# Weight splits ordered behind activation splits at five stage ends of a two-layer trunk

## The chip, the core and the metric

The kernel runs on one core of a Trainium2 chip. The metric is the device time of one launch in microseconds (us); the kernel before takes 1660.06 us, the median of three runs. Engine names in the profile: PE is TensorE (matrix products and transposes), ACT is ScalarE, DVE is VectorE, POOL is GpSimd, SP is SyncE, which here only starts transfers from memory.

## What is computed

The input x has 256 tokens of 1024 float32 values. Two layers follow, each with three residual steps:

```
x = x + 0.5 * RMSNorm_post(SwiGLU_1(RMSNorm_pre(x)))
x = x +       RMSNorm_post(HybridMixer(RMSNorm_pre(x)))
x = x + 0.5 * RMSNorm_post(SwiGLU_2(RMSNorm_pre(x)))

swiglu(u) = (silu(u @ Wg) * (u @ Wu)) @ Wout          # 1024 -> 2 x 2816 -> 1024
HybridMixer(u): proj = u @ W_in, three branches (gated linear recurrence, retention with
  four heads, short convolution), each projected to 1024, summed with sigmoid gates, @ W_out
RMSNorm(x) = x * rsqrt(mean(x*x) + 1e-6) * g
```

So there are six stages in a row, FFN, mixer, FFN, FFN, mixer, FFN, and five places where one stage ends and the next begins. Each stage needs the whole normalised row of x before its first product.

## The kernel before, in words

All 256 tokens stay on the chip as two blocks of 128 rows, called tb 0 and tb 1. Only the weights are streamed in. They come in units of 128 x 1024 values, in one fixed order for the whole kernel, two units to a transfer of 1 MB.

Products are made in a split form: each operand is cut into a rounded high part and a low part that is the rest. `mm3` (lines 397 to 400) then makes three products that add up in one PSUM tile: activation high by weight high (line 398), activation high by weight low (399), activation low by weight high (400). So both weights and activations have to be split first:

- A weight unit is split in `Stream.prep`: ScalarE casts it to `whi` (line 155) and VectorE subtracts to get `wlo` (line 156). There are 8 buffers each for `whi` and `wlo`, and 3 for `raw`, each holding two units. `Stream.done` gives finished units back, and `fill` at once writes down the transfers, casts and subtractions of as many new units.
- Activations are turned by TensorE's transposes into a PSUM tile `pstr` (two of them, used in turn), and `split` casts on ScalarE (line 383) and subtracts on VectorE (line 384). For a stage's input the results are `uh` and `ul`, in two halves of four blocks each (`split_T`). For the last product of an FFN they are the two halves of `hl`.

An FFN step has 11 slices of 256 hidden columns. `fin` makes a slice's gate and up parts, `ftr` turns and splits the result, `fout` multiplies it with the output weights into `acc`. Of the last slice, e, the end of `ffn` goes in this order: for tb 0 `post` scales the sum and adds it to x, and `after` (which is `pre`) makes the next stage's normalised row: multiply by the gain (line 308), row scale, multiply (line 311). Then for tb 1 `fin(e)`, `fout(e-1)`, `ftr(e)`; then `turn`, the transposes of tb 0 for the next stage; `fout(e)`; and `post` and `pre` of tb 1. The transposes of tb 1 are made inside the next stage, at the sixth of eight steps of its second group of products (`inproj`, `KD - 3`).

A row scale (`rstd`) is squares on ScalarE (line 288), a sum on VectorE (line 292) and a power on GpSimd (line 293).

The end of a mixer is alike: `mix_out` multiplies with the last weights, four times for each tb, and `turn` of tb 0 stands inside the last one of tb 1.

In what follows n0 to n7 are the first eight weight units of the next stage. They take the buffers that the last units of the ending stage give back. In an FFN, n0 to n3 follow `fin(e, 1)`, n4 and n5 `fout(e-1, 1)`, n6 and n7 `fout(e, 1)`. In a mixer, two units follow each of the four `mix_out` of tb 1. The next stage's first group of products takes n0 to n3, its second n4 to n7, first for tb 0 and then for tb 1.

Each engine works through its own queue in order. The order in the queues is not that of the program text: a planner places every instruction when the program is built, on the free engine the ready one of highest priority first, by its own estimates of times. Priority is the place in the text; `high_priority(offset=CHAIN_LEAD)` moves an instruction ahead by 150 places.

Of the kernel before, what the change touches and what calls it, by code (L numbers as in the profile page):

```python
# [3 lines left out]

# [1 line left out]

# [5 lines left out]
F32 = mybir.dt.float32  # L12
# [3 lines left out]
ALU = mybir.AluOpType  # L16
# [103 lines left out]
class Stream:  # L120


    def __init__(self, nc, wpool, w, spare):
        self.nc, self.pool, self.w, self.spare = nc, wpool, w, spare
        self.plan = stream_plan()
        self.n = len(self.plan)
        self.next = 0
        self.pair = 0
        self.odd = False
        self.tiles = {}  # L130
        self.cur = 0
# [8 lines left out]
    def prep(self):  # L140
        nc, i = self.nc, self.next
        kind = self.plan[i]
        n = UW // 2 if i < FIRST else UW
        if kind is None:
            if not self.odd:
                self.raw = self.load(n if i < FIRST else 2 * UW)
            k0 = UW if self.odd else 0
            self.odd = not self.odd
            raws = [self.raw[:, k:k + n] for k in range(k0, k0 + UW, n)]
        else:  # L150
            raws = self.part(*kind)
        hi = self.pool.tile([P, UW], F32R, tag="whi", name=f"whi{i}", bufs=WBUFS)
        lo = self.pool.tile([P, UW], F32R, tag="wlo", name=f"wlo{i}", bufs=WBUFS)
        for k, raw in zip(range(0, UW, n), raws):
            nc.scalar.copy(hi[:, k:k + n], raw)  # L155
            nc.vector.tensor_sub(lo[:, k:k + n], raw, hi[:, k:k + n].bitcast(F32))  # L156
        self.tiles[i] = (hi, lo)
        self.next += 1

# [19 lines left out]
    def fill(self):  # L179
        lowest = min(self.tiles) if self.tiles else self.next  # L180
        while self.next < self.n and self.next - lowest < WBUFS:
            self.prep()

    def take(self, n):
        r = list(range(self.cur, self.cur + n))
# [15 lines left out]
def trunk_kernel(ctx: ExitStack, tc: tile.TileContext, x_in, pos, gains, gain0, par, id_in, consts, gw, w, out):  # L201
# [75 lines left out]
            return w4()  # L277
        return tp.tile([P, UW], F32, tag="spl", name=nm("gw"), bufs=7)

    st = Stream(nc, wp, w, spare)  # L280

    def rstd(parts, n, f=1.0):

# [15 lines left out]
    def halves(t):  # L299
        return [t[:, k * 512:(k + 1) * 512] for k in range(2)]  # L300

    def pre(tb, l, k, summed):


        xs = halves(x[tb])
        t = w4()
        for o, a, g in zip(halves(t), xs, halves(gain_tiles[(l, k)])):
            dve.tensor_mul(o, a, g)
        r = rstd([x[tb]], D)
        for o in halves(t):  # L310
            dve.tensor_scalar(o, o, r, None, op0=ALU.mult)

        def turn():
            split_T(tb, t, summed=summed)
        return turn


    sums = [None] * 2
# [2 lines left out]
    def sum_T(tb, j, pt):  # L321
        if tb == 0:
            if j == 0:
                whole[0] = w4()
            act.copy(whole[0][:, j * 512:(j + 1) * 512], pt)
        else:
            make_sums(j, whole[0][:, j * 512:(j + 1) * 512], pt)
# [12 lines left out]
    def split_T(tb, t, scale=None, summed=False):  # L340
        h = tp.tile([P, KD, P], F32R, tag=f"uh{tb}", name=nm("uh"))
        lo = tp.tile([P, KD, P], F32R, tag=f"ul{tb}", name=nm("ul"))
        uh[tb], ul[tb] = h, lo
        for j in range(2):
            pt = ps_tr()
            for i in range(4):
                c = 4 * j + i
                pe.transpose(pt[:, i * P:(i + 1) * P], t[:, c * P:(c + 1) * P], ident)  # L348
            with tc.high_priority(offset=CHAIN_LEAD):
                split(h[:, 4 * j:4 * j + 4, :], lo[:, 4 * j:4 * j + 4, :],  # L350
                      pt.rearrange("p (a b) -> p a b", a=4), scale)
            if summed:
                sum_T(tb, j, pt)

    def first(tb):

# [24 lines left out]
    def split(h, lo, src, scale=None):  # L381
        if scale is None:
            act.copy(h, src)  # L383
            dve.tensor_sub(lo, src, h.bitcast(F32))  # L384
        else:
            act.mul(h, src, scale)
            dve.scalar_tensor_tensor(lo, src, scale, h.bitcast(F32), op0=ALU.mult, op1=ALU.subtract)

    def post(tb, acc, l, k, f):
        r = rstd(acc, D, f)  # L390
# [11 lines left out]
    def inproj(us, tb, turn=None):  # L402

        ps = ps_in()
        for c in range(KD):
            if c == KD - 3 and turn is not None:
                turn()
            h, lo = st.get(us[c // 2])
            s = slice((c % 2) * 512, (c % 2 + 1) * 512)
            mm3(ps, uh[tb][:, c, :], ul[tb][:, c, :], h[:, s], lo[:, s], c == 0, c == KD - 1)  # L410
        return ps
# [20 lines left out]
    def ffn(l, kpost, after, turn, during=None, start=False):  # L432
# [6 lines left out]
        acc = [ps_acc() for _ in range(NTB)]  # L439

        def fin(s, tb, turn=None):
            gate_up(s, tb, [inproj(ui[s], tb, turn)])

        def gate_up(s, tb0, pss):
            for tb, ps in enumerate(pss, tb0):
                t = tok()
                with tc.high_priority(offset=CHAIN_LEAD if s == NS - 1 else 0):
                    act.activation(t[:, 0:256], ps[:, 0:256], AF.Silu)
                    dve.tensor_mul(t[:, 256:512], ps[:, 256:512], t[:, 0:256])
                hT[(s, tb)] = t  # L450

        def ftr(s, tb):
            t = hT[(s, tb)]
            pt = ps_tr()
            for i in range(2):
                pe.transpose(pt[:, i * P:(i + 1) * P], t[:, 256 + i * P:256 + (i + 1) * P], ident)  # L456
            hl = tp.tile([P, 2, 256], F32R, tag=("tmp", "tok")[tb], name=nm("hl"), bufs=(TMP, TOK)[tb])
            with tc.high_priority(offset=CHAIN_LEAD if s == NS - 1 else 0):
                split(hl[:, 0, :], hl[:, 1, :], pt[:, 0:256])
            hT[(s, tb)] = hl  # L460

        def fout(s, tb, ns=(0, 1)):
            hl = hT[(s, tb)]
# [120 lines left out]
        fout(e, 0)  # L584
        with tc.high_priority(offset=CHAIN_LEAD):
            post(0, acc[0], l, kpost, 0.5)
            turn = after(0)
        fin(e, 1)
        st.done(ui[e])
        fout(e - 1, 1)  # L590
        st.done(uo[e - 1])
        ftr(e, 1)
        if turn is not None:
            turn()
        fout(e, 1)
        st.done(uo[e])
        with tc.high_priority(offset=CHAIN_LEAD):
            post(1, acc[1], l, kpost, 0.5)
            return after(1)


    cosT = cp.tile([P, SEQ], F32, tag="cosT", name="cosT")
# [71 lines left out]
    def mixer(l, after, turn):  # L674
# [385 lines left out]
        def mix_out(tb, i, ns=(0, 1)):  # L1060
            outproj(macc[tb], [(uh[tb][:, j, :], ul[tb][:, j, :]) for j in (i, i + 1)],
                    umo[i:i + 2], i == 0, i == 6, ns)
# [4 lines left out]
                split_T(1, M[1], 0.5)  # L1067
        with tc.high_priority(offset=CHAIN_LEAD):
            post(0, macc[0], l, G_MPOST, 1.0)
            turn = after(0)  # L1070
        for i in range(0, 8, 2):
            mix_out(1, i, (0,))
            if i == 6:
                turn()
            mix_out(1, i, (1,))
            st.done(umo[i:i + 2])
        with tc.high_priority(offset=CHAIN_LEAD):
            post(1, macc[1], l, G_MPOST, 1.0)
            return after(1)


    first(0)
# [161 lines left out]
```

## Time and profile before

| what | value |
|---|---|
| median of three runs | 1660.06 us (1659.83 to 1660.34) |
| profiled execution | 1659.72 us |
| its span, first to last instruction | 1657.9 us |
| TensorE busy | 1643.6 us, 99% of the span |
| VectorE busy | 1245.4 us, 75% |
| ScalarE busy | 921.0 us, 56% |
| granted TensorE clock, mean | 0.998 |

The span is the time from the first to the last recorded instruction; the profiled execution has 1.8 us outside it. Matrix products overlap in TensorE, so a product of 0.39 us can start every 0.23 us; a gap in TensorE's work is therefore read from one start to the next and not from the busy time.

### The profile page before, as it was taken

What the parts mean: (1) busy time and instruction counts of PE and PEld (TensorE: products, weight loads), DVE (VectorE), ACT (ScalarE), POOL (GpSimd) and SP (SyncE); (2) the same over time, 40 slices, a digit from 0 to 9 for tenths busy, and PEclk for the clock granted to TensorE, in tenths of its full rate; (3) what the DMA queues carried; (4) which work ended last, traced back from release to release, by engine and by line L of the source; (5) the groups of instructions that cost most, each with busy time, mean ns of one, the idle gap of its engine ahead of it and who ended that gap; (6) DMA issues with size and microseconds to landing.
All of it is one profiled execution on the core that took longest, in us unless ns stands there. A gap on an engine that the chain in (4) does not pass through costs nothing.

```text
span 1657.9 us, 19700 instructions
## 1 busy us (share of the span) xinstructions
PE 1643.6 (99%) x7561; PEld 1354.4 (82%) x7561; DVE 1245.4 (75%) x1594; ACT 921.0 (56%) x1247; POOL 47.3 (3%) x71
## 2 busy tenths in 40 slices
PE   8999999999999999999999999999999999999998
PEld 6888788888888888888888888888888888888886
DVE  7878769976665657888689787798566566678784
ACT  6555567644544545655556555766445544465553
POOL 0030000000000000000000000000000000000000
PEclk9999999999999999999999999999999999999999
DMA  8553554555454465474465344645554454644621
GB/s 336 210 206 127 204 190 165 203 206 189 167 181 175 171 232 223 150 252 161 170 253 187 138 164 163 220 157 203 199 189 171 160 196 153 251 176 177 221 107 71
DMA packets 49774, 309.85 MB, mean 187 GB/s; under 512 B 5648, under 2 KB 6032, under 8 KB 17552
## 3 DMA queue, kind: packets, MB, share of 16 engines
q1 hardware_dynamic: 47376, 301.18, 49.6%
q10 hardware_dynamic: 2304, 7.41, 1.2%
q8 instruction: 59, 0.97, 0.2%
q14 instruction: 35, 0.29, 0.0%
HBM read 307.52 MB, written 1.05 MB: 186 GB/s over the span
## 4 chain that ended last, share of the span: by engine, by line
PE 95%; DVE 3%; issue 1%; POOL 1%; ACT 1%; DMA 0%; SPq 0%; DVEq 0%; POOLq 0%; ACTq 0%
PE psin L400 21%; PE psin L398 21%; PE psin L399 21%; PE psacc L400 9%; PE psacc L398 9%; PE psacc L399 9%; PE pstr L456 1%; DVE wlo L156 1%; PE pstr L713 1%; POOL small L293 1%; PE pstr L348 1%; DVE x L395 0%; PE pstr L881 0%; PE pstr L960 0%; DMA raw<-in_w_dram 0%
## 5 line engine op out<-in xcount | busy, mean ns | idle before, releaser
L156 DVE TENSOR_TENSOR wlo<-raw,whi 128x1024 fp32r<-128x1024 f32 (+1 forms) x506 | 603.7, 1215 | 250.0 <-ACT whi L155 241.6
L155 ACT CAST whi<-raw 128x1024 fp32r<-128x1024 f32 (+1 forms) x506 | 521.6, 1049 | 262.7 <-PE psacc L400 147.5
L398 PE MATMUL psin<-whi,uh 128*128 128x512 f32 x1440 | 567.7, 394 | 1.3 <-ACT uh L383 0.7
L400 PE MATMUL psin<-whi,ul 128*128 128x512 f32 x1440 | 562.5, 391 | 1.8 <-DVE ul L384 1.3
L399 PE MATMUL psin<-wlo,uh 128*128 128x512 f32 x1440 | 563.1, 391 | 0.0
L400 PEld LDWEIGHTS psin<-whi,ul 128*128 128x128 f32 x1440 | 270.6, 188 | 59.0 <-DVE ul L384 2.1
L398 PEld LDWEIGHTS psin<-whi,uh 128*128 128x128 f32 x1440 | 270.8, 188 | 57.4 <-ACT uh L383 2.0
L399 PEld LDWEIGHTS psin<-wlo,uh 128*128 128x128 f32 x1440 | 270.9, 188 | 53.4
L398 PE MATMUL psacc<-whi,hl 128*128 128x512 f32 x352 | 140.8, 400 | 0.8 <-ACT hl L383 0.5
L156 DVE TENSOR_TENSOR wlo<-gw,whi 128x1024 fp32r<-128x1024 f32 x96 | 115.9, 1219 | 30.6 <-ACT whi L155 30.6
L400 PE MATMUL psacc<-whi,hl 128*128 128x512 f32 x352 | 137.4, 392 | 0.0
L399 PE MATMUL psacc<-wlo,hl 128*128 128x512 f32 x352 | 137.4, 390 | 0.0
L155 ACT CAST whi<-gw 128x1024 fp32r<-128x1024 f32 x96 | 101.1, 1053 | 45.5 <-PE psin L400 24.9
L400 PE MATMUL psacc<-whi,spl 128*128 128x512 f32 x256 | 100.0, 391 | 0.0
L398 PE MATMUL psacc<-whi,spl 128*128 128x512 f32 x256 | 99.8, 390 | 0.0
L399 PE MATMUL psacc<-wlo,spl 128*128 128x512 f32 x256 | 99.7, 389 | 0.0
L400 PEld LDWEIGHTS psacc<-whi,hl 128*128 128x128 f32 x352 | 66.1, 188 | 15.2 <-DVE hl L384 1.3
L398 PEld LDWEIGHTS psacc<-whi,hl 128*128 128x128 f32 x352 | 66.1, 188 | 15.1 <-ACT hl L383 3.3
L399 PEld LDWEIGHTS psacc<-wlo,hl 128*128 128x128 f32 x352 | 66.2, 188 | 12.6
L293 POOL TENSOR_TENSOR small<-small,mhalf 128x1 f32<-128x1 f32 x40 | 28.9, 723 | 1534.6 <-DVE small L292 1533.7
L383 ACT CAST hl<-pstr 128x256 fp32r<-128x256 f32 x88 | 31.7, 370 | 56.5 <-PE pstr L456 56.5
L701 ACT COPY tok<-psin 128x512 f32<-128x512 f32 x40 | 23.5, 586 | 62.7 <-PE psin L400 62.7
(191 smaller groups left out, 1686.1 us busy)
## 6 DMA issues: line engine op xcount, KB each, us to landing
raw<-in_w_dram SPq DMA_DIRECT2D x251, 1024.0 KB, 4.8
gw<-in_w_dram SPq DMA_DIRECT2D x48, 512.0 KB, 6.9
w<-in_w_dram SPq DMA_DIRECT2D x16, 512.0 KB, 6.5
gain<-in_gains_dram ACTq DMA_DIRECT2D x10, 512.0 KB, 5.2
w<-in_gw_dram ACTq DMA_DIRECT2D x4, 512.0 KB, 3.5
x<-in_x_dram SPq DMA_DIRECT2D x2, 512.0 KB, 4.2
raw<-in_w_dram SPq DMA_DIRECT2D x4, 256.0 KB, 6.1
out_dram<-x SPq DMA_DIRECT2D x4, 256.0 KB, 2.0
```

Source lines behind the costliest of these rows:

```text
L155: nc.scalar.copy(hi[:, k:k + n], raw)
L156: nc.vector.tensor_sub(lo[:, k:k + n], raw, hi[:, k:k + n].bitcast(F32))
L293: pool_e.tensor_tensor(r, r, mhalf, op=ALU.pow)
L348: pe.transpose(pt[:, i * P:(i + 1) * P], t[:, c * P:(c + 1) * P], ident)
L383: act.copy(h, src)
L398: pe.matmul(ps, lhsT=xh, rhs=wh, start=first, stop=False)
L399: pe.matmul(ps, lhsT=xh, rhs=wl, start=False, stop=False)
L400: pe.matmul(ps, lhsT=xl, rhs=wh, start=False, stop=last)
L456: pe.transpose(pt[:, i * P:(i + 1) * P], t[:, 256 + i * P:256 + (i + 1) * P], ident)
L701: act.copy(t, ps)
L713: pe.transpose(pt[:, i * SEQ + tb * P:i * SEQ + (tb + 1) * P], toks[tb][:, c * P:(c + 1) * P], ident)
```

## The change

`tc.issue_after(ins)` is a block: every instruction written in it for the engine of `ins` gets an edge that puts it behind `ins` in that engine's queue. All the `ins` used here are VectorE's, so the edges bind VectorE's instructions alone; ScalarE's casts and the transfers of the same block are not bound, though they move to another place in the text.

- FFN end: `done(ui[e])` and `done(uo[e-1])` move from behind `fin(e, 1)` and `fout(e-1, 1)` to behind `ftr(e, 1)`, and the six `wlo` subtractions (n0 to n5) come behind the subtraction of `hl` (line 384).
- FFN end: `pre` is cut in two, and its last part (line 311) for tb 0 comes behind the product of gate and up (line 449) of `fin(e, 1)`.
- FFN end: `post` and `pre` of tb 1 come, on VectorE, behind the `wlo` subtraction of n3 (`behind(3)`).
- Mixer end: `done` of units 2 to 5 of the output weights moves behind `turn`, and the subtractions n2 to n5 come behind the last subtraction of `ul`. Units 0 and 1 (n0, n1) stay where they were.

```diff
--- before.py
+++ after.py
@@ -1,6 +1,6 @@
 import math
 from collections import deque
-from contextlib import ExitStack
+from contextlib import ExitStack, nullcontext
 
 import numpy as np
 
@@ -120,8 +120,9 @@
 class Stream:
 
 
-    def __init__(self, nc, wpool, w, spare):
-        self.nc, self.pool, self.w, self.spare = nc, wpool, w, spare
+    def __init__(self, tc, wpool, w, spare):
+        self.tc, self.nc, self.pool, self.w, self.spare = tc, tc.nc, wpool, w, spare
+        self.lows = {}
         self.plan = stream_plan()
         self.n = len(self.plan)
         self.next = 0
@@ -153,7 +154,7 @@
         lo = self.pool.tile([P, UW], F32R, tag="wlo", name=f"wlo{i}", bufs=WBUFS)
         for k, raw in zip(range(0, UW, n), raws):
             nc.scalar.copy(hi[:, k:k + n], raw)
-            nc.vector.tensor_sub(lo[:, k:k + n], raw, hi[:, k:k + n].bitcast(F32))
+            self.lows[i] = nc.vector.tensor_sub(lo[:, k:k + n], raw, hi[:, k:k + n].bitcast(F32))
         self.tiles[i] = (hi, lo)
         self.next += 1
 
@@ -181,6 +182,10 @@
         while self.next < self.n and self.next - lowest < WBUFS:
             self.prep()
 
+    def behind(self, k):
+
+        return self.tc.issue_after(self.lows[self.cur + k].ins) if self.cur + k < self.n else nullcontext()
+
     def take(self, n):
         r = list(range(self.cur, self.cur + n))
         self.cur += n
@@ -277,7 +282,7 @@
             return w4()
         return tp.tile([P, UW], F32, tag="spl", name=nm("gw"), bufs=7)
 
-    st = Stream(nc, wp, w, spare)
+    st = Stream(tc, wp, w, spare)
 
     def rstd(parts, n, f=1.0):
 
@@ -307,12 +312,16 @@
         for o, a, g in zip(halves(t), xs, halves(gain_tiles[(l, k)])):
             dve.tensor_mul(o, a, g)
         r = rstd([x[tb]], D)
-        for o in halves(t):
-            dve.tensor_scalar(o, o, r, None, op0=ALU.mult)
+
+        def scale(behind=None):
+
+            with tc.issue_after(behind.ins) if behind is not None else nullcontext():
+                for o in halves(t):
+                    dve.tensor_scalar(o, o, r, None, op0=ALU.mult)
 
         def turn():
-            split_T(tb, t, summed=summed)
-        return turn
+            return split_T(tb, t, summed=summed)
+        return scale, turn
 
 
     sums = [None] * 2
@@ -347,10 +356,11 @@
                 c = 4 * j + i
                 pe.transpose(pt[:, i * P:(i + 1) * P], t[:, c * P:(c + 1) * P], ident)
             with tc.high_priority(offset=CHAIN_LEAD):
-                split(h[:, 4 * j:4 * j + 4, :], lo[:, 4 * j:4 * j + 4, :],
-                      pt.rearrange("p (a b) -> p a b", a=4), scale)
+                last = split(h[:, 4 * j:4 * j + 4, :], lo[:, 4 * j:4 * j + 4, :],
+                             pt.rearrange("p (a b) -> p a b", a=4), scale)
             if summed:
                 sum_T(tb, j, pt)
+        return last
 
     def first(tb):
 
@@ -381,10 +391,9 @@
     def split(h, lo, src, scale=None):
         if scale is None:
             act.copy(h, src)
-            dve.tensor_sub(lo, src, h.bitcast(F32))
-        else:
-            act.mul(h, src, scale)
-            dve.scalar_tensor_tensor(lo, src, scale, h.bitcast(F32), op0=ALU.mult, op1=ALU.subtract)
+            return dve.tensor_sub(lo, src, h.bitcast(F32))
+        act.mul(h, src, scale)
+        return dve.scalar_tensor_tensor(lo, src, scale, h.bitcast(F32), op0=ALU.mult, op1=ALU.subtract)
 
     def post(tb, acc, l, k, f):
         r = rstd(acc, D, f)
@@ -439,15 +448,16 @@
         acc = [ps_acc() for _ in range(NTB)]
 
         def fin(s, tb, turn=None):
-            gate_up(s, tb, [inproj(ui[s], tb, turn)])
+            return gate_up(s, tb, [inproj(ui[s], tb, turn)])
 
         def gate_up(s, tb0, pss):
             for tb, ps in enumerate(pss, tb0):
                 t = tok()
                 with tc.high_priority(offset=CHAIN_LEAD if s == NS - 1 else 0):
                     act.activation(t[:, 0:256], ps[:, 0:256], AF.Silu)
-                    dve.tensor_mul(t[:, 256:512], ps[:, 256:512], t[:, 0:256])
+                    m = dve.tensor_mul(t[:, 256:512], ps[:, 256:512], t[:, 0:256])
                 hT[(s, tb)] = t
+            return m
 
         def ftr(s, tb):
             t = hT[(s, tb)]
@@ -456,8 +466,9 @@
                 pe.transpose(pt[:, i * P:(i + 1) * P], t[:, 256 + i * P:256 + (i + 1) * P], ident)
             hl = tp.tile([P, 2, 256], F32R, tag=("tmp", "tok")[tb], name=nm("hl"), bufs=(TMP, TOK)[tb])
             with tc.high_priority(offset=CHAIN_LEAD if s == NS - 1 else 0):
-                split(hl[:, 0, :], hl[:, 1, :], pt[:, 0:256])
+                last = split(hl[:, 0, :], hl[:, 1, :], pt[:, 0:256])
             hT[(s, tb)] = hl
+            return last
 
         def fout(s, tb, ns=(0, 1)):
             hl = hT[(s, tb)]
@@ -584,19 +595,27 @@
         fout(e, 0)
         with tc.high_priority(offset=CHAIN_LEAD):
             post(0, acc[0], l, kpost, 0.5)
-            turn = after(0)
-        fin(e, 1)
-        st.done(ui[e])
+            r = after(0)
+        m = fin(e, 1)
+        if r is not None:
+            with tc.high_priority(offset=CHAIN_LEAD):
+                r[0](m)
         fout(e - 1, 1)
-        st.done(uo[e - 1])
-        ftr(e, 1)
-        if turn is not None:
-            turn()
+
+        with tc.issue_after(ftr(e, 1).ins):
+            st.done(ui[e])
+            st.done(uo[e - 1])
+        if r is not None:
+            r[1]()
         fout(e, 1)
         st.done(uo[e])
-        with tc.high_priority(offset=CHAIN_LEAD):
+
+        with tc.high_priority(offset=CHAIN_LEAD), st.behind(3):
             post(1, acc[1], l, kpost, 0.5)
-            return after(1)
+            r = after(1)
+            if r is not None:
+                r[0]()
+                return r[1]
 
 
     cosT = cp.tile([P, SEQ], F32, tag="cosT", name="cosT")
@@ -1067,16 +1086,23 @@
                 split_T(1, M[1], 0.5)
         with tc.high_priority(offset=CHAIN_LEAD):
             post(0, macc[0], l, G_MPOST, 1.0)
-            turn = after(0)
-        for i in range(0, 8, 2):
-            mix_out(1, i, (0,))
-            if i == 6:
-                turn()
-            mix_out(1, i, (1,))
-            st.done(umo[i:i + 2])
+            scale, turn = after(0)
+            scale()
+        for i in range(0, 6, 2):
+            mix_out(1, i)
+            if i == 0:
+                st.done(umo[i:i + 2])
+        mix_out(1, 6, (0,))
+
+        with tc.issue_after(turn().ins):
+            st.done(umo[2:6])
+        mix_out(1, 6, (1,))
+        st.done(umo[6:8])
         with tc.high_priority(offset=CHAIN_LEAD):
             post(1, macc[1], l, G_MPOST, 1.0)
-            return after(1)
+            scale, turn = after(1)
+            scale()
+            return turn
 
 
     first(0)
```

## Rows read from the trace of the kernel before

**Rows 1.** The page, part 1: busy time, share of the span, instructions

```profile
PE 1643.6 (99%) x7561; PEld 1354.4 (82%) x7561; DVE 1245.4 (75%) x1594; ACT 921.0 (56%) x1247; POOL 47.3 (3%) x71
```

**Rows 2.** The chain that ended last, first mixer's end: start us, us, what

```profile
646.72 3.45 DVE wlo L156 x4
```

**Rows 3.** Timeline, TensorE, first FFN end: start, us, engine, line, operation [idle before]

```profile
193.09 0.39 PE L400 MATMUL psacc<-whi,hl 128*128 128x512 f32 x1
193.66 0.44 PE L456 MATMUL pstr<-ident,tok 128*128 128x128 f32 x2 [0.18 <-DVE tok L449]
...
194.61 0.50 PE L398 MATMUL psacc<-whi,hl 128*128 128x512 f32 x1
...
195.41 0.40 PE L399 MATMUL psacc<-wlo,hl 128*128 128x512 f32 x1
196.04 0.50 PE L398 MATMUL psin<-whi,uh 128*128 128x512 f32 x1 [0.24 <-ACT uh L383]
...
198.68 0.40 PE L399 MATMUL psin<-wlo,uh 128*128 128x512 f32 x1
198.91 0.39 PE L400 MATMUL psin<-whi,ul 128*128 128x512 f32 x1
```

**Rows 4.** Timeline, VectorE, the same end

```profile
189.52 1.22 DVE L156 TENSOR_TENSOR wlo<-raw,whi 128x1024 fp32r<-128x1024 f32 x1
...
193.51 2.35 DVE L156 TENSOR_TENSOR wlo<-raw,whi 128x1024 fp32r<-128x1024 f32 x2
195.78 0.42 DVE L384 TENSOR_TENSOR hl<-pstr,hl 128x256 fp32r<-128x256 f32 x1
...
199.58 0.69 DVE L393 TENSOR_TENSOR w<-psacc,gain 128x512 f32<-128x512 f32 x1
...
203.62 1.21 DVE L156 TENSOR_TENSOR wlo<-raw,whi 128x1024 fp32r<-128x1024 f32 x1
...
206.47 0.88 DVE L311 TENSOR_SCALAR w<-w,small 128x512 f32<-128x512 f32 x2 [0.44 <-POOL small L293]
```

**Rows 5.** Timeline, ScalarE, the same end

```profile
191.07 0.37 ACT L448 ACTIVATE tok<-psin 128x256 f32<-128x256 f32 x1
...
192.88 1.05 ACT L155 CAST whi<-raw 128x1024 fp32r<-128x1024 f32 x1 [0.49 <-ACT whi L155]
194.19 0.37 ACT L383 CAST hl<-pstr 128x256 fp32r<-128x256 f32 x1 [0.26 <-PE pstr L456]
```

**Rows 6.** Timeline, TensorE, the next transposes behind that end

```profile
207.30 1.03 PE L348 MATMUL pstr<-ident,w 128*128 128x128 f32 x8
208.09 0.47 PE L398 MATMUL psin<-whi,uh 128*128 128x512 f32 x1
```

**Rows 7.** Timeline, TensorE, the first mixer's end

```profile
650.87 0.39 PE L398 MATMUL psin<-whi,uh 128*128 128x512 f32 x1
651.91 0.50 PE L400 MATMUL psin<-whi,ul 128*128 128x512 f32 x1 [0.65 <-DVE ul L384]
```

**Rows 8.** Timeline, VectorE, the first mixer's end

```profile
646.63 4.62 DVE L156 TENSOR_TENSOR wlo<-raw,whi 128x1024 fp32r<-128x1024 f32 x4
651.17 1.28 DVE L384 TENSOR_TENSOR ul<-pstr,uh 128x512 fp32r<-128x512 f32 x2
```

**Rows 9.** Timeline, ScalarE, the first mixer's end

```profile
648.86 1.08 ACT L383 CAST uh<-pstr 128x512 fp32r<-128x512 f32 x2 [0.49 <-PE pstr L348]
```

**Rows 10.** Windows, FFN, mixer end: length; busy PE, PEld, DVE, ACT, POOL; clock, DMA

```profile
193.10:207.40 14.30, 13.80 (x64) 10.75 (x63) 13.74 (x21) 8.11 (x14) 2.01 (x2) 1.00 0.76 294
...
646.70:660.40 13.70, 13.05 (x63) 10.45 (x62) 12.88 (x20) 8.40 (x15) 1.10 (x2) 1.00 0.89 333
```

**Rows 11.** Timeline, GpSimd: two of the powers of the row scales

```profile
190.88 1.47 POOL L293 TENSOR_TENSOR small<-small,mhalf 128x1 f32<-128x1 f32 x1 [3.93 <-DVE small L292]
...
658.96 0.55 POOL L293 TENSOR_TENSOR small<-small,mhalf 128x1 f32<-128x1 f32 x1 [3.49 <-DVE small L292]
```

**Rows 12.** The page, part 6: transfers of raw weights, KB each, us to landing

```profile
raw<-in_w_dram SPq DMA_DIRECT2D x251, 1024.0 KB, 4.8
```

## The prediction

> **What bounds the kernel now.** I read the page's busy times first. TensorE works 99% of the span, and no other engine comes near [rows 1]. So a change can gain only what TensorE's queue stands still, and can lose by adding stops to it. The chain that ended last shows where to look: nearly all of it is products, but at the first mixer's end 3.45 us of weight subtractions, four in a row, stand on it [rows 2]. Then I went through TensorE's timeline at each of the five stage ends, from start to start. In steady work a product starts every 0.23 us (198.68 to 198.91) and eight transposes take 0.79 us (207.30 to 208.09), 0.1 us each [rows 3, 6].
>
> At the first FFN end, from the last product of `fout(e-1, 1)` at 193.09 to 198.68, TensorE starts 14 products and 10 transposes. They need 14 x 0.227 + 10 x 0.099 = 4.17 us and take 5.59, so 1.42 us is lost [rows 3]. The reader sees where: the transposes of `ftr` wait for line 449, the first product with `hl` starts nearly a microsecond after them, and behind 195.41 `hl`'s low part is missing and only a product of the next stage fills in. VectorE shows why. Its subtraction of `hl` starts at 195.78, behind two weight subtractions that fill 193.51 to 195.86 [rows 4]. There are three such ends (that of the last FFN has no next stage and no units); I take them as equal. At a mixer's end TensorE has 1.04 us between two starts, 0.81 too much, waiting for `ul` [rows 7]. ScalarE had begun `uh` at 648.86 and needs 0.54 for a half, but VectorE was in its four weight subtractions until 651.2 [rows 8, 9]. There are two such ends.
>
> **What the change removes.** FFN end: `silu` ends at 191.44 [rows 5], so line 449 can be done by 191.9 and the scaling (line 311) behind it by 192.8, before TensorE finishes `fout(e-1, 1)` at 193.09 + 0.23 = 193.32. The transposes then start without a wait. ScalarE's cast of `hl` began 0.53 behind the first transpose (193.66 to 194.19) and TensorE went on 0.42 behind the cast's start [rows 3, 5]; from 193.32 that gives 194.27, while its six transposes end at 193.91. A wait of about 0.39 stays, and `hl`'s low part, with no weight subtraction ahead of it, is in time. Removed: 1.42 - 0.39 = 1.03 us, three times 3.09. Mixer end: `ul`'s first half can start at 649.4 and be done by 650.1, before TensorE wants it at 651.10. Removed: 0.81, twice 1.62. Together 4.71 us, the most that I can find.
>
> **What it adds: VectorE has no room there.** The edges take no work away. In an FFN end n0 was split at 189.52 and n1 right after [rows 4], while VectorE waited for squares and for the power. Now they wait for `hl` and fall into the stretch from there to the transposes of tb 1 at 207.30. In that stretch (193.10 to 207.40, 14.30 us) VectorE was busy 13.74 us already [rows 10]. After the change the stretch ends 1.03 earlier and VectorE idles at its start until `hl`'s cast is nearly done, at 194.27: 14.30 - 1.03 - 1.17 = 12.1 us remain. The work is 13.74 + 2 x 1.13 (n0, n1) - 0.41 (the end of lines 311 and 449 moves out) = 15.6. It is 3.5 us too much. In a mixer end the stretch 646.70 to 660.40 has 12.88 us of work in 13.70. It ends 0.81 earlier, and VectorE idles from 646.7 until `uh` is there at 649.4: 10.2 us remain, 2.7 too little.
>
> Being late on VectorE is not yet a stop of TensorE. Of three products only the second reads `wlo`, and the planner does take others first, as it did with the product of the next stage at 196.04 [rows 3]. Behind the place of tb 1's transposes stand nine products of the same group, of which six don't need a late `wlo` (6 x 0.227 = 1.4 us), and then the next group of tb 1, whose units n0 to n3 are long split; I take as much again from it. That covers 2.8 us. The FFN end keeps 3.5 - 2.8 = 0.7, from bounds of 0 (all covered) and 3.5 (nothing covered). The mixer end's 2.7 are just covered, but its power for tb 1 (658.96) now runs in 0.55, and beside a weight subtraction such powers take 1.47 [rows 11]. If a subtraction falls beside it, the path is 0.9 longer; I take half, 0.45, bounds 0 and 2.7 + 0.9 = 3.6. Given back: 3 x 0.7 + 2 x 0.45 = 3.0 us.
>
> The Trainium skill has a rule on this (SBUF — State Buffer, Who interferes with whom): a VectorE instruction with both inputs in SBUF and a GpSimd instruction that reads SBUF exclude each other for the whole of whichever starts first. The rows of 0.55 and 1.47 agree. By the rule alone a power could wait up to a whole subtraction, 1.22 us in the trace; at both mixers that would be 2 x 1.22 = 2.4 us instead of my 0.9, and the sum 1.5 us worse.
>
> Costed at nothing: the casts on ScalarE, which have no edge, as long as they don't go ahead of `hl` (a rival below). And the transfers: the buffer of n0 and n1 comes free after n1's subtraction, some 5 us later in an FFN end, so that the transfer for n6 and n7 starts about 197 and not 192. With 4.8 us to land [rows 12] it is there at 202, and its first product is due at about 197.4 + 36 x 0.227 = 205.6; a cast and a subtraction (1.05 + 1.22) fit between. Without that cover each microsecond later would be one more of stop. `post` of tb 1 behind n3 costs nothing apart from the sum over the stretch: n3 is done at about 194.3 + 0.3 + 4 x 1.13 + 1.2 = 200.3, and `post` began at 199.58 before [rows 4].
>
> **The sum.** 4.7 removed, 3.0 given back: 1.7 us less, 1658.0 for the profiled execution's 1659.72. The median is 0.34 above that execution, so 1658.3.
>
> **The rivals.**
> A. Nothing is given back. The planner sees the late units and gives TensorE other products. For it: the filled-in product at 196.04. Against: 3.5 us too much work in a stretch without slack. 1660.06 - 4.7 = 1655.4.
>
> B. Slower: n4 starves. The edge protects n0 to n3 alone, and `post` and `pre` of tb 1, with their lead of 150, come before n4. They took VectorE from 199.58 to the first unit at 203.62 [rows 4], so 4.0 us; from 200.3 that is 204.3, and n4 is split at 205.5. TensorE wants it at 197.4 + 24 x 0.227 + 0.23 = 203.1. If it stands there in order, it loses 2.4 us and gains 1.03: 1.4 worse at each FFN end, 4.2 for three; with the same order at the mixers, where the chain is tied to nothing, 0.81 gained against 1.2 lost, 0.8 for two. Sum +5: 1665. It decides from a new wait of more than 1.03 us at the first product that reads n4's `wlo`. Against: four of a unit's six products read only `whi`.
>
> C. It doesn't do what it says. ScalarE's casts are not bound, and the cast of n5, about ready at 193.6, may be queued ahead of `hl`; a cast takes 1.05 [rows 5] and undoes the 1.03 at an FFN end. With the mixers' 0.36 x 2 left, and no more than that given back elsewhere: 1659.5.
>
> **How the numbers follow.** My forecast 0.52, A 0.22, C 0.15, B 0.11. About 0.2%, 3.3 us, is what a measurement of this kernel can tell from no change, so faster means below 1656.7 and slower above 1663.4. A, and a little of my forecast's lower side (0.03), is faster: 0.25. Most of B is slower: 0.08. The rest, 0.67, is no change. The likeliest case's own range is 1656.5 to 1660, from half and from nearly one and a half of what I take as given back. The range for 8 in 10 reaches down to A and up into B: 1655.2 to 1661.8.
>
> **What would show it.** Right: at the FFN ends no stop between 193.1 and the transposes, `hl`'s subtraction straight behind its cast, `ul` at the mixers' ends straight behind `uh`, VectorE idle ahead of both, and then new small waits of TensorE, 0.3 to 1 us each, for `wlo` of n4 to n7 or for `uh` of tb 1. Wrong: none of these new waits (A), one of over a microsecond at n4 (B), or a cast between the transposes of `ftr` and `hl` (C). A wait of `whi` for its transfer at n6 would show the cover of the transfer gone.

## The result: slower by 10.6 us, and the profile after

The changed kernel takes 1670.69 us (median of 4 runs, 1670.48 to 1670.77) against 1660.13 (1659.83 to 1660.34): the ratio is 1.0063 [1.0051, 1.0075]. The forecast was 1658.3 in a range of 1655.2 to 1661.8. It was wrong in sign and outside the range. The profiled execution took 1670.77 us, with a span of 1669.0 where it was 1657.9.

The page, part 1, of the changed kernel, against [rows 1]: TensorE's and VectorE's busy times hardly differ, so the time went into stops.

```profile
PE 1646.3 (99%) x7561; PEld 1355.7 (81%) x7561; DVE 1245.7 (75%) x1594; ACT 921.2 (55%) x1247; POOL 46.5 (3%) x71
```

TensorE's waits by cause, changed kernel (line waiting, what it waited for, us in total, times, longest). Line 408 is the product that reads a low part `wlo`, 157 the subtraction that makes it, 297 a tiny operation of VectorE that happened to end last before the product started, just behind the subtraction:

```profile
PE psin L408 <- DVE small L297: 6.1, 3, 2.1
PE psin L408 <- DVE wlo L157: 4.8, 6, 2.1
```

These 10.9 us were not there before. The timelines show where, at the first FFN end (lines 407, 408 and 409 are the old 398, 399 and 400, line 357 the old 348, 466 the old 456). TensorE, changed kernel, against [rows 3 and 6]:

```profile
193.17 0.39 PE L409 MATMUL psacc<-whi,hl 128*128 128x512 f32 x1
193.41 0.38 PE L466 MATMUL pstr<-ident,tok 128*128 128x128 f32 x2
193.62 0.60 PE L357 MATMUL pstr<-ident,w 128*128 128x128 f32 x4
194.34 0.50 PE L407 MATMUL psacc<-whi,hl 128*128 128x512 f32 x1
...
203.08 0.39 PE L407 MATMUL psin<-whi,uh 128*128 128x512 f32 x1
205.52 0.50 PE L408 MATMUL psin<-wlo,uh 128*128 128x512 f32 x1 [2.05 <-DVE small L297]
...
208.38 0.60 PE L357 MATMUL pstr<-ident,w 128*128 128x128 f32 x4
209.18 0.50 PE L408 MATMUL psin<-wlo,uh 128*128 128x512 f32 x1 [0.20 <-DVE wlo L157]
...
210.10 0.47 PE L407 MATMUL psin<-whi,uh 128*128 128x512 f32 x1
```

The 25th and 26th product of the next stage, the first two that read unit n4, in the kernel before:

```profile
203.90 0.39 PE L398 MATMUL psin<-whi,uh 128*128 128x512 f32 x1
204.13 0.39 PE L399 MATMUL psin<-wlo,uh 128*128 128x512 f32 x1
```

Read by product: the end starts 0.08 us later than before (193.17 against 193.09), but product 25 starts at 203.08 instead of 203.90. So the change did gain 0.90 us. Then TensorE stands: product 26 is 1.39 later than before, which is 2.21 lost in one place. Product 40, the first behind the transposes of tb 1 (208.09 in [rows 6], now 210.10), is 2.01 later; 0.62 more went at a second, small wait and the split transposes around it. Net of the 0.08, this end costs 1.93.

VectorE at the same end, changed kernel, against [rows 4] (line 394 is `hl` and `ul`; 402, 404 and 313 are `post` and `pre` of tb 1):

```profile
194.31 0.42 DVE L394 TENSOR_TENSOR hl<-pstr,hl 128x256 fp32r<-128x256 f32 x1 [1.53 <-ACT hl L393]
194.66 1.22 DVE L157 TENSOR_TENSOR wlo<-raw,whi 128x1024 fp32r<-128x1024 f32 x1
195.79 1.29 DVE L394 TENSOR_TENSOR ul<-pstr,uh 128x512 fp32r<-128x512 f32 x2
197.00 3.48 DVE L157 TENSOR_TENSOR wlo<-raw,whi 128x1024 fp32r<-128x1024 f32 x3
...
200.52 1.28 DVE L402 TENSOR_TENSOR w<-psacc,gain 128x512 f32<-128x512 f32 x2
201.72 1.41 DVE L404 SCALAR_TENSOR_TENSOR x<-w,small,x 128x512 f32<-128x512 f32 x2
203.04 1.29 DVE L313 TENSOR_TENSOR w<-x,gain 128x512 f32<-128x512 f32 x2
204.25 1.22 DVE L157 TENSOR_TENSOR wlo<-raw,whi 128x1024 fp32r<-128x1024 f32 x1
```

The stop's cause is in these lines. `hl` is now first, behind an idle gap of 1.53 us. All four units n0 to n3 follow it, then the chain of tb 1, and n4's subtraction runs from 204.25 to 205.47, where product 26 needed it at about 203.3. Windows of the changed kernel (length; busy PE, PEld, DVE, ACT, POOL; clock, DMA) show the same as sums:

```profile
190.00:194.31 4.31, 4.22 (x22) 3.34 (x20) 1.37 (x4) 3.82 (x8) 0.56 (x1) 1.00 0.00 0
194.31:207.10 12.79, 10.72 (x48) 8.58 (x49) 12.35 (x17) 6.88 (x12) 2.01 (x2) 1.00 0.59 231
```

VectorE is busy for 1.37 us of the 4.31 ahead of `hl`, and then for 12.35 of 12.79: two subtractions were pushed out of a stretch where VectorE idles into one where it has no gap.

The mixers' ends look alike. VectorE and then TensorE at the first one, changed kernel, against [rows 7 and 8]:

```profile
651.57 1.29 DVE L394 TENSOR_TENSOR ul<-pstr,uh 128x512 fp32r<-128x512 f32 x2 [2.76 <-ACT uh L393]
...
659.05 1.22 DVE L157 TENSOR_TENSOR wlo<-raw,whi 128x1024 fp32r<-128x1024 f32 x1
```

```profile
657.98 0.39 PE L407 MATMUL psin<-whi,uh 128*128 128x512 f32 x1
660.32 0.50 PE L408 MATMUL psin<-wlo,uh 128*128 128x512 f32 x1 [1.96 <-DVE wlo L157]
```

`ul` no longer holds anything up; n4's low part does, for 1.96 us. The same transposes of a later stage in both traces show how the loss adds up. Before, and then the changed kernel:

```profile
741.60 0.60 PE L456 MATMUL pstr<-ident,tok 128*128 128x128 f32 x4
...
989.08 0.60 PE L456 MATMUL pstr<-ident,tok 128*128 128x128 f32 x4
...
1560.39 0.60 PE L456 MATMUL pstr<-ident,tok 128*128 128x128 f32 x4
```

```profile
745.66 0.60 PE L466 MATMUL pstr<-ident,tok 128*128 128x128 f32 x4
...
995.29 0.60 PE L466 MATMUL pstr<-ident,tok 128*128 128x128 f32 x4
...
1571.46 0.60 PE L466 MATMUL pstr<-ident,tok 128*128 128x128 f32 x4
```

They come 4.06 us later behind one FFN end and one mixer, 6.21 behind the second FFN end, and 11.07 behind all five ends. So the first two ends cost 4.06 together (0.08 of it stood before the first), the second FFN end 2.15, and the last two 4.86; the last section says why those cost more.

### The profile page after: what moved, and what is told of

It is laid out like the page before. It is cut to its first block, busy times and chain, and to the rows that moved or that the text cites. A ratio compares the mean times of both kernels' runs of the same rounds, so it can differ in the third digit from the quotient of the medians.

```text
span 1669.0 us, 19701 instructions
## 1 busy us (share of the span) xinstructions
PE 1646.3 (99%) x7561; PEld 1355.7 (81%) x7561; DVE 1245.7 (75%) x1594; ACT 921.2 (55%) x1247; POOL 46.5 (3%) x71
## 4 chain that ended last, share of the span: by engine, by line
PE 94%; DVE 4%; ACT 1%; issue 1%; POOL 0%; DMA 0%; SPq 0%; DVEq 0%; POOLq 0%; ACTq 0%
PE psin L408 21%; PE psin L409 21%; PE psin L407 20%; PE psacc L407 9%; PE psacc L409 9%; PE psacc L408 9%; DVE wlo L157 2%; PE pstr L466 1%; PE pstr L732 1%; ACT whi L156 1%; PE pstr L357 0%; DVE x L404 0%; PE pstr L979 0%; PE pstr L900 0%; POOL small L298 0%
## 5 line engine op out<-in xcount | busy, mean ns | idle before, releaser
L408 PE MATMUL psin<-wlo,uh 128*128 128x512 f32 x1440 | 564.8, 392 | 10.8 <-DVE small L297 6.1
```

Source lines behind the costliest of these rows:

```text
L408: pe.matmul(ps, lhsT=xh, rhs=wl, start=False, stop=False)
```

## The experiments

Two theories. Backlog: the edge carries VectorE's work past its idle time, and TensorE stops at the first low part that is late. Order: only `post`'s place ahead of n4 is at fault (`st.behind(3)`), and a later place cures it. All diffs are against the changed kernel unless they say otherwise, and show its main lines. Each ratio is against runs of the kernel before that were measured beside the experiment (medians 1660.0 to 1660.5).

**One half at a time.** e1 has the FFN ends of before and the mixer ends of after, e9 the reverse.

```diff
 e1:
-        with tc.issue_after(ftr(e, 1).ins):
-            st.done(ui[e])
-            st.done(uo[e - 1])
+        ftr(e, 1)        # done() again where it stood before
 ...                      # the scaling too, and no behind(3)
 e9:
-        with tc.issue_after(turn().ins):
-            st.done(umo[2:6])
+        turn()           # inside the loop, done() again per pair
```

> The FFN ends as in the kernel before, the mixer ends as in the changed one. Theory 1 (backlog): the edges carry subtractions past VectorE's idle time, VectorE is then late with all that follows, and TensorE, whose queue is in order, stands at the first product that reads n4's low part. Each end then costs what its own markers in the two traces say, 1.9 and 1.7 us for the two mixers: +3.6, 1663.7 us, with two waits of about 2 us and none at the FFN ends. If the ends hang together (transfers or buffers of one end disturb the next) the sum isn't that: under 1661.5 or over 1666.

> The mixer ends as in the kernel before, the FFN ends as in the changed one. If the ends add up (theory 1, each end late by its own backlog): 1670.7 less the 4.7 of the mixer part alone, 1666 us (1665 to 1667), with three waits of about 2 us at n4. If an end disturbs the next, under 1664 or over 1668.

e1 took 1664.78 (1.0028 [1.0017, 1.0039]), e9 1666.6 (1.0036 [1.0022, 1.005]). Over before they are 4.7 and 6.1, and the sum, 10.8, is the whole change's 10.6. Each half makes its own stops at its own ends: three of up to 2.1 us at the first `wlo` product of n4 in e9, two of about 2 us in e1. So the mixers' ends lose too, where I had counted them as all but covered. e1 came out 1.1 above the 1663.7 that I expected; in its traced execution the second mixer's end has the slow clock of the last section, and costs 2.9 where the first costs 1.8.

**Order against backlog.** e2 puts `post` of tb 1 behind n5 instead of n3.

```diff
-        with tc.high_priority(offset=CHAIN_LEAD), st.behind(3):
+        with tc.high_priority(offset=CHAIN_LEAD), st.behind(5):
```

> The changed kernel, but post and pre of tb 1 come behind the subtraction of n5 and not of n3 at the FFN ends. Theory 2 (wrong order only): TensorE stands because the chain of tb 1 was let ahead of n4; with n4 and n5 ahead of it the three waits of 2.2 us and the slow stretch behind the third one (1.2) go: 1663 us. Theory 1 (backlog): VectorE has the same work in the same time, so the wait only moves, from n4's low part to the transposes or activations of tb 1: 1668.5 to 1674 us, with waits of 2 to 3.5 us there.

1669.73 (1668.4 to 1670.23; 1.0054 [1.0037, 1.0071]), no cure. TensorE and then VectorE in e2, first FFN end:

```profile
206.28 0.39 PE L407 MATMUL psin<-whi,uh 128*128 128x512 f32 x1
208.26 0.50 PE L408 MATMUL psin<-wlo,uh 128*128 128x512 f32 x1 [1.60 <-DVE wlo L157]
```

```profile
198.61 4.62 DVE L157 TENSOR_TENSOR wlo<-raw,whi 128x1024 fp32r<-128x1024 f32 x4
...
206.99 2.35 DVE L157 TENSOR_TENSOR wlo<-raw,whi 128x1024 fp32r<-128x1024 f32 x2
```

n4 and n5 are in time now, the chain behind them is late, and the stop has moved to n6. I had expected it at the transposes of tb 1; waits of 0.2 to 0.4 stand there. The order theory falls: in both orders what comes last in VectorE's queue is late.

**The edges alone.** e3 keeps the new order of the text and the scaling behind line 458, and ties no subtraction to `hl` or `ul`.

```diff
-        with tc.issue_after(ftr(e, 1).ins):
+        ftr(e, 1)
+        if True:
             st.done(ui[e])
 ...
-        with tc.issue_after(turn().ins):
+        turn()
+        if True:
             st.done(umo[2:6])
```

> The changed kernel with its text in the new order, but without the edges on the weight subtractions (those of behind(3) and of the scaling behind line 449 stay). Theories 1 and 2: VectorE uses its idle time again, no wait at n4; 1659 to 1660.5 us. Theory 3 (place in the text): the later place of done lowers the priority of casts and transfers and starves n4: over 1666 us, the wait at n4 stays.

1659.34 (0.9994 [0.9985, 1.0004]): no difference from before that can be told, and no wait at n4. VectorE in e3, first FFN end:

```profile
193.04 2.35 DVE L157 TENSOR_TENSOR wlo<-raw,whi 128x1024 fp32r<-128x1024 f32 x2
195.31 0.42 DVE L394 TENSOR_TENSOR hl<-pstr,hl 128x256 fp32r<-128x256 f32 x1
```

The two subtractions are ahead of `hl` again, as in [rows 4]. So the loss hangs on the edges, not on the text's order. Of the gain, 0.3 to 0.4 us per FFN end is there without them in e3's trace, since line 458 ends at 192.13 and the transposes behind it no longer wait; the rest of the 0.9 needs the edge.

**How many units must be free.** e4, e6 and e5 give back the first three, two and one units of an FFN end before the edge; the mixers' n0 to n3 are free in all three.

```diff
         m = fin(e, 1)
+        st.done(ui[e][:k])               # k = 3 (e4), 2 (e6), 1 (e5)
 ...
-            st.done(ui[e])
+            st.done(ui[e][k:])
 ...
-            if i == 0:
+            if i <= 2:                   # e5, e6: written otherwise, same units
                 st.done(umo[i:i + 2])
 ...
-            st.done(umo[2:6])
+            st.done(umo[4:6])
```

> The changed kernel, but the units that fit VectorE's idle time are given back before the edge: n0 to n2 at FFN ends, n0 to n3 at mixer ends; n3 to n5 and n4, n5 stay behind hl and ul. Theory 1: nothing is carried past idle time, so what the edge removes is kept at the FFN ends, about 1 us each, and the mixers come out between -0.8 and +1 each, as n6 and n7 may fall into the chain of tb 1 there: 1655.5 to 1659.5 us. Theory 2: post and pre still go ahead of later units, waits of about 2 us stay at the first unit behind them: over 1665 us.

> The same with n0 and n1 given back before the edge at the FFN ends. Theory 1: the wait at n4 is gone or under 0.3 us (2.05 - 2 x 1.13 is below zero), a smaller one of up to 1 us may stand at n6, whose subtraction is still behind the chain; 1657 to 1660.5 us. The order of the queue is again the same at n4 (behind line 313), so if order alone counts: about 2 us at n4, 1663 us or more.

> As the run in which n0 to n2 (FFN) and n0 to n3 (mixer) are given back before the edge, but at the FFN ends only n0 is. Theory 1 (backlog): the lateness goes by about one subtraction, 1.13 us, per unit that is put past the idle time. With none free the FFN ends cost 5.9 us together (1670.7 less 1664.8), with three free they gain. With one free the wait at the first late unit should be about 2.05 - 1.13 = 0.9 us and the sum lie between, 1660 to 1664 us. If instead the chain of tb 1 ahead of n4 is all that counts, the order of the queue there is unchanged (n4 still stands behind line 313), and the wait stays about 2 us: 1663 us or more.

Measured: three free 1657.19 (0.9982 [0.9972, 0.9991]), two free 1659.77 (0.9998 [0.9989, 1.0007]), one free 1662.58 (1.0017 [1.0007, 1.0026]). The second unit is worth 2.8 us over the three ends, the third 2.6: 0.9 per end each. The wait at n4 goes with it: 2.05 with none free (e9), 0.9 with one, 0.2 with two, none with three; a second wait of 0.2, at n6, goes with the third unit too. The first unit takes 1.15 us off the wait, about what one subtraction takes (1.13 to 1.22). This is the backlog, in units of a subtraction. The wait in e5:

```profile
204.07 0.50 PE L408 MATMUL psin<-wlo,uh 128*128 128x512 f32 x1 [0.89 <-DVE wlo L157]
```

And VectorE in e4, first FFN end:

```profile
193.23 1.22 DVE L157 TENSOR_TENSOR wlo<-raw,whi 128x1024 fp32r<-128x1024 f32 x1
194.36 0.42 DVE L394 TENSOR_TENSOR hl<-pstr,hl 128x256 fp32r<-128x256 f32 x1
...
202.52 1.22 DVE L157 TENSOR_TENSOR wlo<-raw,whi 128x1024 fp32r<-128x1024 f32 x1
...
205.38 0.88 DVE L320 TENSOR_SCALAR w<-w,small 128x512 f32<-128x512 f32 x2 [0.44 <-POOL small L298]
```

A third subtraction fits exactly into the gap that the edge left empty: it starts at 193.23 and `hl` at 194.36, only 0.05 later than 194.31. The edge keeps its gain and costs nothing here. The scaling for tb 1 ends at 206.26, ahead of its transposes (206.44).

**What is left.** In e4, a wait of 0.43 and one of 0.40 us stay at the mixers' transposes of tb 1, and at the FFN ends the wait ahead of `hl`'s first product, 0.3 us as in the changed kernel. e7 frees the mixers' n4 too; e8 also puts the transposes of `ftr(e, 1)` between the halves of `fout(e - 1, 1)`.

```diff
 e7, against e4:
-            if i <= 2:
-                st.done(umo[i:i + 2])
+            st.done(umo[i:min(i + 2, 5)])
 ...
-            st.done(umo[4:6])
+            st.done(umo[5:6])
 e8, against e7:
-        fout(e - 1, 1)
-        with tc.issue_after(ftr(e, 1).ins):
+        fout(e - 1, 1, (0,))
+        hs = ftr(e, 1)
+        fout(e - 1, 1, (1,))
+        with tc.issue_after(hs.ins):
```

> n0 to n2 free at FFN ends as before, and at mixer ends n4 too, so that only n5 waits for ul there. VectorE's idle time ahead of uh is 2.7 us, three subtractions need 3.4: ul would start some 0.7 later, but TensorE wants it 1.6 us later than uh can be there, so no wait; and one subtraction less falls between the sums and line 311 of tb 1, where the run with n0 to n3 free had a wait of 0.43. Theory 1: 0.4 us better per mixer, 1656.4 us (1655.8 to 1657). If ul is late after all, a wait at its first product and 1657.2 or more.

> The run with n0 to n2 and n0 to n4 free, and the transposes of ftr(e, 1) moved between the two halves of fout(e-1, 1), so that ScalarE casts hl while TensorE still has six products. The 0.37 us by which TensorE stands before hl's first product at each FFN end goes: 3 x 0.35 = 1 us less than the run without it, 1655.4 us. Rival: line 449 is done only at about 192, as late as the first half of fout(e-1, 1), so that TensorE stands there for up to as much, and VectorE, with hl earlier, loses the room for n2: no gain, 1656.4 or more.

1656.94 (0.9982 [0.9973, 0.999]) and 1656.79 (0.998 [0.9971, 0.9988]): both beat before, neither can be told from e4. e7's mixers still wait 0.5 at the transposes, where I had expected the 0.4 to go: three subtractions (3.49 us) don't fit into the 2.76 ahead of `ul`, and the chain of tb 1 starts later. In e8 the wait ahead of `hl`'s first product is gone, but only 0.15 of the 1 us that I expected from it came. The rival stated beside it came out. e8's first FFN end, from the last product of gate and up to the first of the next stage, takes 7.24 us (190.27 to 197.51), in e7 7.19 (190.59 to 197.78): TensorE is 0.14 late at the transposes of `ftr`, as line 458 ends only at 192.18, 0.13 at the second four of tb 0, and loses 0.09 behind the one group of transposes more. At the second FFN end a wait of 0.2 for the scaling of tb 1 is new.

**TensorE's order.** If the queue stops because one `wlo` product stands in the way, products that read only `whi` could go first. e10 is the changed kernel with the second group's products so written; e11 does that to e8.

```diff
-            mm3(ps, ...)                 # per c; turn() at KD - 3
+        for c, h, lo in steps:           # 16 products that read whi
+            pe.matmul(ps, lhsT=uh[tb][:, c, :], rhs=h, ...)
+            pe.matmul(ps, lhsT=ul[tb][:, c, :], rhs=h, ...)
+        turn()
+        for c, h, lo in steps:           # then the 8 that read wlo
+            pe.matmul(ps, lhsT=uh[tb][:, c, :], rhs=lo, ...)
```

> The changed kernel with all its edges, but in the second group of products of a stage (the one that holds the transposes of tb 1) the eight products that read wlo are written behind the sixteen that read whi, and the transposes between them. Theory 1, its second half: VectorE's lateness becomes a stop only because TensorE's queue has a product with wlo of n4 in second place. With 3.6 us of other products ahead of it the waits at n4 go, smaller ones stay at whi of n6 (its transfer starts late) and at the transposes, about 1.2 us per end instead of 2.65: 1662.5 to 1666 us. If it isn't the place in TensorE's queue (VectorE's lateness reaches TensorE through the activations of tb 1 anyway), the waits move there and the time stays over 1668.5.

> The best so far (n0 to n2 and n0 to n4 free, ftr between the halves of fout, 1656.8 us) with the same reordering of the second group. No product with wlo stands late there, so little is left to cover: the wait of 0.5 at a mixer's transposes shrinks by at most one product's 0.23, and 1656.0 to 1657 us. If products in this order cost anything by themselves (the weights of whi loaded twice in a row, sums ended later), over 1657.5.

e10: 1665.88 (1.0033 [1.0021, 1.0045]), 4.8 us less than the changed kernel (5.2 when each is taken against its own runs of the kernel before). Its waits on TensorE:

```profile
PE psin L428 <- DVE wlo L157: 3.1, 2, 1.6
...
PE pstr L357 <- DVE w L320: 1.6, 5, 0.5
...
PE psin L424 <- ACT whi L156: 0.9, 3, 0.3
```

No wait at n4 is left. In its place come the mixers' last unit n7 (1.55 each), the transposes of tb 1, and `whi` of n6, which nobody had waited for before; once, 0.9 us for line 467, the product of gate and up, which VectorE did only behind n7 and `ul`. So the order in TensorE's queue decided where it stopped, and the backlog, later in the group, still costs about half: the first and third FFN end now cost 0.3 each, the second 1.9 with that last wait, the mixers still 1.7 and 1.5. With the backlog gone (e11, 1656.68; 0.9977 [0.9967, 0.9986]) the order brings nothing over e8's 1656.79 that these runs can tell. e11 is the best version run; e4 to e11's 0.5 us is not a difference that these runs can tell.

## Why the prediction was wrong, step by step

**What is removed: right.** At an FFN end I had 1.03 and the runs show 0.90 at product 25; a wait of about 0.39 was to stay ahead of `hl`'s first product, and 0.32 did (194.34, behind four transposes of 0.1 each from 193.62). `hl`'s subtraction is straight behind its cast: ScalarE, changed kernel, against [rows 5].

```profile
192.96 1.05 ACT L156 CAST whi<-raw 128x1024 fp32r<-128x1024 f32 x1 [0.49 <-ACT whi L156]
193.92 0.37 ACT L393 CAST hl<-pstr 128x256 fp32r<-128x256 f32 x1
```

The 0.39 is by my own times 0.36 (194.27 - 193.91). At the mixers the wait for `ul` is gone, and TensorE is 0.9 us ahead when it reaches n4's low part. But not all of the 4.7 can be kept: e4, without the backlog at the FFN ends, measures 2.9 us, 0.8 to 0.9 per FFN end and 0.2 and 0.4 at the mixers.

**VectorE's backlog: right in kind and nearly in size.** I had 3.5 us too much at an FFN end and 2.7 at a mixer's. An FFN end lost 2.21 and 0.62 behind product 25, 2.8 in all. The first mixer's end, from the transposes of tb 0 (648.17, now 650.26) to the first product behind those of tb 1 (661.00, now 664.90), cost 1.81 net and had gained 0.9, so 2.7 were lost there.

**The cover of 2.8 us: this step failed.** "The planner does take others first" was read off one product, the one filled in at 196.04 [rows 3]. At n4 in the changed kernel it takes none: product 26 is n4's `wlo` as written, and one product, 25, stands ahead of it, 0.23 us. (At n6 it takes four transposes first, and TensorE still stands.) That most of a group's products don't need a late `wlo` helps nothing when they stand behind one that does; e10 wrote them ahead and got 4.8 us back. I had also put the late unit in the wrong place: the edge makes n4 late, the first unit of its group, and my cover was counted behind the transposes of tb 1, where the rest of n6 and n7 are read. With the cover at 0.2 instead of 2.8, my own terms give 3.3 back per FFN end and about 3.4 per mixer (2.7 - 0.2 + 0.9): 16.7 - 4.7 = +12, against 10.6 measured, of which about 1.1 in the traced execution is the slow clock of the last section.

**Rival B was the mechanism, at a chance of 0.11.** Its place, n4's first `wlo` product, and its condition, a wait over 1.03 us, came out at all five ends; it had 2.4 for the stop and 2.21 was lost. It missed three things: the second wait at n6 (0.62 at the first FFN end), the mixers (1.2 assumed, a wait of 1.96 measured), and the slow clock below. I had held against it that four of six products read only `whi`, the same error as the cover.

**Rivals A and C were not seen.** All of the gain was given back and more. The cast ahead of `hl` started before the transposes, as in the kernel before. (C's 1659.5 is a slip: 1660.06 less its 2 x 0.36 is 1659.3.) The cover for the transfers held, though the transfer of n6 and n7 was issued at 198.28 and not about 197: at n4 and n6 it was the subtraction that came last; only e10 waits for `whi`, 0.3 us.

**The powers: right at the mixers, and hidden in the changed kernel.** GpSimd at the first FFN end: the late power of the kernel before (the early one is in [rows 11]), then both of the changed kernel.

```profile
204.97 1.46 POOL L293 TENSOR_TENSOR small<-small,mhalf 128x1 f32<-128x1 f32 x1 [3.93 <-DVE small L292]
```

```profile
190.58 0.56 POOL L298 TENSOR_TENSOR small<-small,mhalf 128x1 f32<-128x1 f32 x1 [3.54 <-DVE small L297]
...
205.60 1.46 POOL L298 TENSOR_TENSOR small<-small,mhalf 128x1 f32<-128x1 f32 x1 [4.37 <-DVE small L297]
```

Here only the early power changes, from 1.47 to 0.56, now that no subtraction runs beside it; the late one takes 1.46 in both, beside n5's subtraction (205.44 to 206.66) in the changed kernel. At the first mixer the late one went from 0.55 to 1.40, as feared. No transposes waited for it in the changed kernel, since the stop at n4 had made them later still. In e4, without that stop, they do: the power takes 1.40 (from 657.59), VectorE idles 0.45 for it ahead of the scaling, and TensorE waits 0.43, about the 0.45 that I had taken; no run has the power alone changed. The Trainium skill's rule (SBUF — State Buffer, Who interferes with whom), that a VectorE instruction with two inputs in SBUF and a reading GpSimd instruction exclude each other, fits these times.

## What to carry to other kernels

An edge that orders an engine's work also moves work over that engine's idle time: before tying work behind a critical instruction, sum what the engine did in the gap ahead of it, and tie only what doesn't fit there. A late operand stops an in-order queue at its first reader, so cover is what stands ahead of that reader in the queue, and not all the work that could be done without it.

## What the runs showed of the hardware

A stop can have an after-effect that I had not expected. Windows of the changed kernel around the stop of the third FFN end (length; busy PE, PEld, DVE, ACT, POOL; clock, DMA), and TensorE's timeline there:

```profile
1029.50:1031.00 1.50, 0.78 (x3) 0.67 (x4) 1.50 (x3) 1.50 (x3) 0.62 (x1) 1.00 0.93 347
1031.32:1034.31 2.99, 2.99 (x9) 2.30 (x8) 2.55 (x5) 0.12 (x1) 0.46 (x1) 0.50 0.91 325
1034.40:1037.00 2.60, 2.60 (x17) 2.14 (x16) 1.41 (x3) 1.17 (x2) 0.00 (x0) 0.96 0.84 280
```

```profile
1027.79 0.39 PE L407 MATMUL psin<-whi,uh 128*128 128x512 f32 x1
1030.22 0.50 PE L408 MATMUL psin<-wlo,uh 128*128 128x512 f32 x1 [2.05 <-DVE wlo L157]
...
1031.32 0.63 PE L409 MATMUL psin<-whi,ul 128*128 128x512 f32 x1
1031.75 0.63 PE L407 MATMUL psin<-whi,uh 128*128 128x512 f32 x1
```

TensorE stood for 2.05 us, started again at the full clock, and a microsecond later the granted clock was 0.50, which is the 1.2 GHz level, for 3 us. Seven products from 1031.32 then start 0.43 apart and not 0.23: 7 x 0.2 = 1.4 us. The second wait, at n6, is missing at this end, so that it costs 3.05 net, 1.1 more than the 1.9 of the other two FFN ends. The four other stops at n4 in that execution, 1.96 to 2.05 us long, left the clock at 1.00. The same happened once in e1 (0.50 from 1481 to 1484) and once in e2 (0.55 from 1485 to 1488), and at none of e9's three stops of 2.05. Nor does it take the change: the kernel before has 0.50 from 10.0 to 13.4 us of its span, behind a wait of 1.92 us, while e1, with 2.84 us at that place, keeps 1.00. What decides whether it falls stays open.
